# Gamma on GpSimd and VectorE ahead of the root, and three stores instead of four, in the last row block of a matmul with RMS norm

## The chip, the cores and the metric

One core of one Trainium2 chip. The profile is one execution of the program. Its engines are TensorE (PE), VectorE (DVE), ScalarE (ACT), GpSimd (POOL) and SyncE (SP, which here issues stores). In the text, **R** is the start of the last reciprocal in the trace, the moment from which everything still to do is scaling and storing. "R+4.95" is 4.95 us after it. A packet is one piece that a DMA engine moves; a store has landed when its completion has reached its semaphore, the counter that SP waits on. "The root" is the square root of the mean square of a row, and r its reciprocal.

## The reference

```python
m, k, n = 2048, 2048, 2048
x = np.matmul(a, b)
rms = np.sqrt(np.mean(x ** 2, axis=-1, keepdims=True) + eps)
return (gamma * x / rms).astype(np.float32)
```

## The kernel before

The kernel forms the product in groups of two row blocks of 128 rows, with seven block products for each half of the columns in place of eight (a Strassen scheme). A row block can leave only when its whole row of 2048 columns is known, because the root needs the sum of all its squares. For the last block, `rb`, that is after the last matmul, so everything from there to the last byte in the output is exposed. The columns are named by chunks of 512: chunks 0 and 1 are the halves of the tile `xb`, chunk 2 is `p4[1]` (in PSUM, the memory that the matmuls write), chunk 3 is `x22[1]`; `x22[0]` is chunk 1.

```python
        product(g, 0, 6, p6)
        add(x22[0], p6, t[0])                # chunk 1 of the last block
        square(rb, x22[0])
        # ... (first row block is stored here; chunk 2 becomes complete in p4[1])
        for h, col in enumerate(halves):     # chunk 3, in two halves, after the last matmuls
            add(x22[1][:, col], p6[h], t[1][:, col])
            # ... ACT squares this half and sums it into half_sq[:, h]
        part = stat_pool.tile([P, 1], FP32, name="part")
        nc.vector.tensor_scalar(out=part, in0=half_sq[:, 0:1], scalar1=pre_b,
                                scalar2=msq[rb][:, 2:3], op0=ALU.add, op1=ALU.add)
        add(x22[0], x22[0], gam[1], ALU.mult)          # chunk 1 times gamma
        r_b = inverse_rms(half_sq[:, 1:2], part)       # ACT root, VectorE reciprocal
        x = xb[:, 0:CH]
        nc.vector.tensor_scalar_mul(out=x, in0=x, scalar1=r_b)
        nc.sync.dma_start(out=rows(rb, 0, CH), in_=x)
        x = xb[:, CH:]
        by_r(x, r_b)                                   # ACT scales chunk 1
        nc.scalar.dma_start(out=rows(rb, CH, HALF), in_=x)
        for c, x, src in ((3, x22[1], x22[1]), (2, x21[1], p4[1])):
            scaled_gamma(x, src, r_b, gam[c])          # times r and gamma, one operation
            nc.sync.dma_start(out=rows(rb, c * CH, (c + 1) * CH), in_=x)
```

So four stores of 256 KB leave, in rows of 2 KB per partition.

Of the kernel before, what the change touches and what calls it, by code (L numbers as in the profile page):

```python
# [8 lines left out]
FP32 = mybir.dt.float32  # L9
# [4 lines left out]
ALU = mybir.AluOpType  # L14
# [3 lines left out]
def kernel(  # L18
# [13 lines left out]
    nc = tc.nc  # L32
    P = 128
    M, K = a.shape
    _, N = b.shape
# [4 lines left out]
    CH = 512  # L40
    NCH = N // CH
    HALF = N // 2
# [6 lines left out]
    a_pool = ctx.enter_context(tc.tile_pool(name="a_pool", bufs=2))  # L49
# [60 lines left out]
    a32 = {}  # L110
# [156 lines left out]
    def b_quarter(j, kp, r, c):  # L267
        return raw[j][kp][:, r, c * CH:(c + 1) * CH]
# [24 lines left out]
    def product(g, j, m, bank, start=True, within={}):  # L293
        for kp in range(KP):
            for work in within.get(kp, ()):
                work()
            product_matmul(g, j, m, bank, kp, start)
# [5 lines left out]
    def square(mb, src):  # L303
        c = n_sq[mb]
        n_sq[mb] += 1
        sq = sq_pool.tile([P, 2 * CH], BF16, name="sq")
        nc.scalar.activation(out=sq[:, 0:CH], in_=src, func=ACTF.Square,  # L307
                             scale=inv_sqrt_n, accum_out=msq[mb][:, c:c + 1])
# [8 lines left out]
    def x_tile(mb, h):  # L317


        if (mb, h) not in x_half:  # L320
            n = n_x[0]
            n_x[0] += 1
            if n < 8:
                slot = n
            else:
                g = n // 4
                slot = ((0, 4, 1, 5), (0, 1, 4, 5))[g // 2 % 2 == 0][n % 4] + 2 * (g % 2)
            x_half[mb, h] = x_slot[slot]
        return x_half[mb, h]

    def x_chunk(mb, c):
        return x_tile(mb, c // 2)[:, (c % 2) * CH:(c % 2 + 1) * CH]
# [15 lines left out]
    def inverse_rms(last, partial):  # L348

        rms = stat_pool.tile([P, 1], FP32, name="rms")  # L350
        nc.scalar.activation(out=rms, in_=last, func=ACTF.Sqrt, bias=partial, scale=1.0)  # L351
        return inverse(rms)

    def rows(mb, lo, hi):
        return out[mb * P:(mb + 1) * P, lo:hi]
# [18 lines left out]
    def finish(mb, order=(0, 1)):  # L374
        for h in order:
            scale(mb, (h,))
            store(mb, (h,))
# [9 lines left out]
    def new_bank():  # L387
        return ps_a.tile([P, CH], FP32, name="acc")
# [121 lines left out]
    x11, x12, x21, x22 = (x_chunk(r, c) for r in (r2, r3) for c in (2, 3))  # L510
# [47 lines left out]
    def last_squares():  # L558

        while late:  # L560
            square(*late.pop(0))
# [121 lines left out]
    def last_group():  # L683


        g = NG - 1
        ra, rb = 2 * g, 2 * g + 1
        x11, x12, x21, x22 = ([x_chunk(mb, 2 * j + c) for j in range(2)]
                              for mb in (ra, rb) for c in range(2))
        xa, xb = x_tile(ra, 0), x_tile(rb, 0)  # L690
        gam = [gamma_sb[:, c * CH:(c + 1) * CH] for c in range(NCH)]
        gam_left = gamma_sb[:, 0:HALF]
        t = x22

        def partial(mb):

            m = msq[mb]
            part = stat_pool.tile([P, 1], FP32, name="part")
            nc.vector.tensor_scalar(out=part, in0=m[:, 0:1], scalar1=m[:, 1:2],
                                    scalar2=m[:, NCH:], op0=ALU.add, op1=ALU.add)  # L700
            return part

        def plus(part, mb, c):
            both = stat_pool.tile([P, 1], FP32, name="both")
            nc.vector.tensor_tensor(out=both, in0=part, in1=msq[mb][:, c:c + 1], op=ALU.add)
            return both

        def add(out, in0, in1, op=ALU.add):
            nc.vector.tensor_tensor(out=out, in0=in0, in1=in1, op=op)  # L709

        def scaled_gamma(x, src, r, gamma_of_x):
            nc.vector.scalar_tensor_tensor(out=x, in0=src, scalar=r, in1=gamma_of_x,  # L712
                                           op0=ALU.mult, op1=ALU.mult)

        def by_r(x, r):
            nc.scalar.activation(out=x, in_=x, func=ACTF.Copy, scale=r)

        p4 = []
        for j in range(2):
            p5, p1 = new_bank(), new_bank()  # L720
            p4.append(new_bank())
            product(g, j, 5, p5)
            nc.scalar.copy(out=t[j], in_=p5)
            last_squares()
            product(g, j, 1, p1)
            add(t[j], p1, t[j], ALU.subtract)
            if j == 0:
                finish(2 * g - 2)
            product(g, j, 4, p4[j])
            nc.scalar.copy(out=x21[j], in_=p4[j])  # L730
            add(x11[j], t[j], x21[j])
            if j == 0:
                finish(2 * g - 1)
            product(g, j, 3, p5, start=False)
            nc.scalar.copy(out=x12[j], in_=p5)
            square(ra, x12[j])
            add(t[j], x11[j], x12[j])
            p7 = new_bank()
            product(g, j, 7, p7)
            add(x11[j], p7, x11[j])  # L740
            square(ra, x11[j])
            if j == 0:
                product(g, j, 2, p4[j], start=False)
                nc.scalar.copy(out=x21[j], in_=p4[j])
                square(rb, x21[j])
                add(t[j], t[j], x21[j], ALU.subtract)
                pre_a = partial(ra)
                add(xa, xa, gam_left, ALU.mult)
                add(x21[j], x21[j], gam[0], ALU.mult)
        r_a = inverse_rms(msq[ra][:, NCH - 1:NCH], plus(pre_a, ra, 2))  # L750
        by_r(xa, r_a)
        nc.sync.dma_start(out=rows(ra, 0, HALF), in_=xa)
        p6 = new_bank()
        product(g, 0, 6, p6)
        add(x22[0], p6, t[0])
        square(rb, x22[0])
        scaled_gamma(x_tile(ra, 1), x_tile(ra, 1), r_a, gamma_sb[:, HALF:])
        nc.sync.dma_start(out=rows(ra, HALF, N), in_=x_tile(ra, 1))
        product(g, 1, 2, p4[1], start=False)
        add(t[1], t[1], p4[1], ALU.subtract)  # L760
        square(rb, p4[1])
        pre_b = partial(rb)

        half_sq = stat_pool.tile([P, 2], FP32, name="n2")
        halves = [slice(0, CH // 2), slice(CH // 2, CH)]
        p6 = [new_bank()[:, 0:CH // 2] for _ in halves]
        for bank, col in zip(p6, halves):
            for kp in range(KP):
                nc.tensor.matmul(bank, s_sum[6][:, kp, :], b_quarter(1, kp, 0, 1)[:, col],
                                 start=(kp == 0), stop=(kp == KP - 1))  # L770
        for h, col in enumerate(halves):
            add(x22[1][:, col], p6[h], t[1][:, col])
            sq = sq_pool.tile([P, 2 * CH], BF16, name="sq")
            nc.scalar.activation(out=sq[:, 0:CH // 2], in_=x22[1][:, col], func=ACTF.Square,  # L774
                                 scale=inv_sqrt_n, accum_out=half_sq[:, h:h + 1])
        part = stat_pool.tile([P, 1], FP32, name="part")
        nc.vector.tensor_scalar(out=part, in0=half_sq[:, 0:1], scalar1=pre_b,
                                scalar2=msq[rb][:, 2:3], op0=ALU.add, op1=ALU.add)
        add(x22[0], x22[0], gam[1], ALU.mult)
        r_b = inverse_rms(half_sq[:, 1:2], part)  # L780
        x = xb[:, 0:CH]
        nc.vector.tensor_scalar_mul(out=x, in0=x, scalar1=r_b)  # L782
        nc.sync.dma_start(out=rows(rb, 0, CH), in_=x)
        x = xb[:, CH:]
        by_r(x, r_b)
        nc.scalar.dma_start(out=rows(rb, CH, HALF), in_=x)
        for c, x, src in ((3, x22[1], x22[1]), (2, x21[1], p4[1])):
            scaled_gamma(x, src, r_b, gam[c])
            nc.sync.dma_start(out=rows(rb, c * CH, (c + 1) * CH), in_=x)

    for g in range(G0, NG - 1):
        for j in range(2):
            group_half(g, j, hooks_of(g, j))
    last_group()

# [33 lines left out]
```

## Time and profile before

| | before |
|---|---|
| time, median of the first 3 runs | 223.0 us |
| span of the profiled execution, granted TensorE clock | 221.1 us, 0.993 |
| R | 214.59 us |
| last store issued | R+2.03 |
| last data packet ends | R+4.95 |
| last store landed | R+5.53 |
| span end | R+6.51 |

The page's busy times (first line) and the engines of the chain that ended last (second line):

```profile
PE 210.4 (95%) x1035; PEld 97.7 (44%) x1035; DVE 167.9 (76%) x330; ACT 128.0 (58%) x263; POOL 26.7 (12%) x56
...
PE 69%; DMA 23%; DVE 2%; POOL 2%; issue 1%; ACT 1%; DVEq 0%; ACTq 0%; POOLq 0%
```
The kernel is bound by TensorE: 95% busy. The change does not touch that part. What it touches is the last 8 us, seen in the timeline of the kernel before (columns: start, duration, engine, line of the kernel, operation, output<-input, shapes):

```profile
213.16 0.42 DVE L709 TENSOR_TENSOR x<-acc,x 128x256 f32<-128x256 f32 x1 [0.27 <-PE acc L769]
...
213.72 0.27 DVE L777 TENSOR_SCALAR part<-n,part,msq 128x1 f32<-128x1 f32 x1
213.91 0.68 DVE L709 TENSOR_TENSOR x<-x,gamma_sb 128x512 f32<-128x512 f32 x1
...
214.26 0.29 ACT L351 ACTIVATE rms<-n,part 128x1 f32<-128x1 f32 x1
214.59 0.16 DVE L345 RECIPROCAL r<-rms 128x1 f32<-128x1 f32 x1
214.79 0.72 ACT L716 ACTIVATE x<-x,r 128x512 f32<-128x512 f32 x1 [0.23 <-DVE r L345]
214.79 0.48 DVE L782 TENSOR_SCALAR x<-x,r 128x512 f32<-128x512 f32 x1
215.19 0.74 DVE L712 SCALAR_TENSOR_TENSOR x<-x,r,gamma_sb 128x512 f32<-128x512 f32 x1
215.30 0.33 SPq L783 DMA_DIRECT2D out_dram<-x  x1
215.54 0.35 ACTq L786 DMA_DIRECT2D out_dram<-x  x1
215.85 0.74 DVE L712 SCALAR_TENSOR_TENSOR x<-acc,r,gamma_sb 128x512 f32<-128x512 f32 x1
215.96 1.05 SPq L789 DMA_DIRECT2D out_dram<-x  x2
```
The second half of chunk 3 comes out of PSUM at 213.16. ACT squares it, and takes the root at 214.26; VectorE forms the partial sum (L777) and multiplies chunk 1 by gamma (L709, 0.68 us) meanwhile. At 214.59 comes the reciprocal (R). Then VectorE scales chunk 0 in 0.48 us, and chunks 3 and 2 with r and gamma together in 0.74 us each. The stores are issued as these end; the last line merges two, at 215.96 and 216.62.

What the DMA engines do after that, in 40 slices of 0.1 us from R+1.41 (busy share in tenths, then GB/s):

```profile
DMA  0689999999989999999699999999795643100000
GB/s 0 205 328 410 451 369 389 348 349 430 410 184 266 307 410 369 369 307 266 164 266 348 348 389 389 389 287 348 246 328 184 266 184 143 41 0 0 0 0 0
```
None of these stores' packets moves before R+1.54, 0.83 us after the first issue. Then the engines are busy for some 3 us, but the rate dips, to 184, 164 and 246 GB/s between stretches of 350 to 410, and it tails off.

The time from issue to landing in the same stretch (columns: tensors, issuing queue, operation, count, size, median us to landing):

```profile
out_dram<-x SPq DMA_DIRECT2D x3, 256.0 KB, 3.5
out_dram<-x ACTq DMA_DIRECT2D x1, 256.0 KB, 3.1
```

### The profile page before, as it was taken

The numbers are of one execution on the slowest core, as the hardware profiler recorded it, in microseconds if no ns is written. First come the engines' busy times: TensorE is split into PE (matmuls) and PEld (weight loads), VectorE is DVE, ScalarE is ACT, GpSimd is POOL, SyncE is SP. The second block draws the span as 40 slices with busy tenths as digits, with TensorE's granted clock in tenths as the row PEclk, the third lists the DMA queues.
The fourth block names the chain that finished last, engine by engine and source line by source line (L and its number), as shares of the span: only waits on it lengthen the run. The fifth ranks groups of instructions, "written<-read, shape, count | busy, mean of one in ns | idle before, by whom it ended". The sixth has DMA issues, their size and how long they took to land.

```text
span 221.1 us, 3017 instructions
## 1 busy us (share of the span) xinstructions
PE 210.4 (95%) x1035; PEld 97.7 (44%) x1035; DVE 167.9 (76%) x330; ACT 128.0 (58%) x263; POOL 26.7 (12%) x56
## 2 busy tenths in 40 slices
PE   7999999999999999999999999999999999999950
PEld 2445445444455444444444444444444444444430
DVE  2428789999978898969696649855794759797691
ACT  3110002920698898578846997299738995334580
POOL 7534232220000002200100002000200000000000
PEclk9999999999999999999999999999999999999997
DMA  6999999999938595946799149945798349044045
GB/s 184 226 203 210 202 208 211 212 211 240 424 113 354 195 294 107 361 189 175 213 320 409 45 88 269 373 205 95 195 312 348 75 89 386 21 190 193 1 191 190
DMA packets 36464, 47.13 MB, mean 213 GB/s; under 512 B 21984, under 2 KB 26080, under 8 KB 35040
## 3 DMA queue, kind: packets, MB, share of 16 engines
q0 software_dynamic: 9936, 23.33, 41.2%
q1 hardware_dynamic: 26080, 22.29, 33.6%
q10 hardware_dynamic: 432, 1.31, 2.1%
q8 instruction: 8, 0.13, 0.2%
q14 instruction: 8, 0.07, 0.1%
HBM read 34.60 MB, written 16.78 MB: 232 GB/s over the span
## 4 chain that ended last, share of the span: by engine, by line
PE 69%; DMA 23%; DVE 2%; POOL 2%; issue 1%; ACT 1%; DVEq 0%; ACTq 0%; POOLq 0%
PE acc L289 67%; DMA b<-in_b_dram 23%; DVE x L709 1%; POOL early L105 1%; DVE x L712 1%; PE acc L384 1%; POOL b L99 1%; ACT sq L307 0%; PE tbank L189 0%; PE acc L189 0%; DVEq L824 0%; ACT sq L774 0%; DVE x L782 0%; DVE r L345 0%; ACT rms L351 0%
## 5 line engine op out<-in xcount | busy, mean ns | idle before, releaser
L289 PE MATMUL acc<-b,s 128*128 128x512 bf16 x408 | 92.1, 379 | 0.2 <-DMA b<-in_b_dram 0.2
L289 PEld LDWEIGHTS <-s 128*128 128x128 f16 (+1 forms) x512 | 49.9, 98 | 60.3 <-issue 0.5
L384 PE MATMUL acc<-b,head_at 128*128 128x512 bf16 x176 | 41.8, 379 | 0.6 <-DMA b<-in_b_dram 0.5
L307 ACT ACTIVATE sq<-x 128x512 bf16<-128x512 f32 x54 | 34.0, 630 | 6.9 <-DVE x L709 3.0
L366 DVE SCALAR_TENSOR_TENSOR x<-x,r,gamma_sb 128x1024 f32<-128x1024 f32 x28 | 34.8, 1281 | 0.7
L223 ACT ACTIVATE sq<-a 128x1024 bf16<-128x1024 f32 x24 | 25.3, 1054 | 2.5 <-DMA a<-in_a_dram 2.0
L384 PEld LDWEIGHTS <-head_at 128*128 128x128 bf16 x176 | 16.8, 98 | 20.1 <-issue 1.2
L246 ACT ACTIVATE head_at<-a,s 128x2048 f16<-128x2048 f32 x10 | 20.0, 1998 | 3.7 <-DVE s L233 3.7
L426 ACT COPY x<-acc 128x512 f32<-128x512 f32 x6 | 3.4, 588 | 25.2 <-PE acc L384 25.2
L289 PEld LDWEIGHTS <-head_at 128*128 128x128 f16 (+1 forms) x112 | 10.9, 98 | 13.2
L289 PE MATMUL acc<-early,head_at 128*128 128x512 bf16 x64 | 14.5, 379 | 0.0
L289 PEld LDWEIGHTS <-at_even 128*128 128x128 f16 x96 | 9.4, 98 | 11.3
L289 PE MATMUL acc<-early,s 128*128 128x512 bf16 x56 | 14.4, 379 | 0.0
L264 DVE TENSOR_TENSOR s<-head_at 128x1024 f16<-128x1024 f16 (+5 forms) x22 | 13.4, 635 | 0.1
L596 DVE TENSOR_TENSOR x<-x,x 128x512 f32<-128x512 f32 x9 | 6.2, 692 | 8.8 <-ACT x L594 8.3
L99 POOL DMA_DIRECT2D b<-in_b_dram x15 | 10.6, 705 | 15.5 <-DMA b<-in_b_dram 13.0
L578 ACT COPY x<-acc 128x512 f32<-128x512 f32 x9 | 5.2, 573 | 11.5 <-PE acc L289 11.5
L289 PE MATMUL acc<-t_left,s 128*128 128x512 bf16 x48 | 11.3, 379 | 0.0
L280 DVE TENSOR_TENSOR b<-b 128x1024 bf16<-128x1024 bf16 x16 | 10.8, 686 | 0.2
L289 PE MATMUL acc<-t_left,at_even 128*128 128x512 bf16 x48 | 10.8, 379 | 0.0
L289 PE MATMUL acc<-early,at_even 128*128 128x512 bf16 x48 | 10.8, 379 | 0.0
L289 PE MATMUL acc<-t_left,head_at 128*128 128x512 bf16 x48 | 10.8, 379 | 0.0
(106 smaller groups left out, 215.0 us busy)
## 6 DMA issues: line engine op xcount, KB each, us to landing
out_dram<-x SPq DMA_DIRECT2D x30, 512.0 KB, 3.9
a<-in_a_dram POOLq DMA_DIRECT2D x10, 1024.0 KB, 8.6
b<-in_b_dram POOLq DMA_DIRECT2D x15, 512.0 KB, 17.0
a<-in_a_dram POOLq DMA_DIRECT2D x4, 512.0 KB, 17.2
early<-in_a_dram POOLq DMA_DIRECT2D x7, 256.0 KB, 14.6
early<-in_b_dram ACTq DMA_DIRECT2D x2, 512.0 KB, 5.9
gamma_sb<-in_gamma_dram POOLq DMA_DIRECT2D x1, 1024.0 KB, 15.3
out_dram<-x SPq DMA_DIRECT2D x3, 256.0 KB, 3.5
```

Of the source, the lines that this page charges most:

```text
L99: nc.gpsimd.dma_start(out=raw[j][kp], in_=b[kp * W2:(kp + 1) * W2, j * HALF:(j + 1) * HALF].rearrange("(t p) n -> p t n", p=P))
L223: nc.scalar.activation(out=junk, in_=a32[mb][:, h * HALF:(h + 1) * HALF], func=ACTF.Square, scale=2.0 ** -8, accum_out=n2[:, h:h + 1])
L246: nc.scalar.activation(out=a16[mb], in_=a32.pop(mb), func=ACTF.Copy, scale=factor.pop(mb))
L264: nc.vector.tensor_tensor(out=sum_of(g, s)[:, lo:hi, :], in0=x[:, lo:hi, :], in1=y[:, lo:hi, :], op=op)
L280: nc.vector.tensor_tensor(out=flat[:, 1:3, :], in0=flat[:, 1:3, :], in1=flat[:, 0::3, :], op=ALU.add)
L289: nc.tensor.matmul(bank, lhsT[:, kp, :], rhs, start=(start and kp == 0), stop=(kp == KP - 1), skip_group_check=not start)
L307: nc.scalar.activation(out=sq[:, 0:CH], in_=src, func=ACTF.Square, scale=inv_sqrt_n, accum_out=msq[mb][:, c:c + 1])
L366: nc.vector.scalar_tensor_tensor(out=x, in0=x, scalar=inverse_of[mb], in1=gamma_sb[:, h * HALF:(h + 1) * HALF], op0=ALU.mult, op1=ALU.mult)
L384: nc.tensor.matmul(bank, head_at[:, kt, r, :], head_rhs(c, kt), start=(kt == 0), stop=(kt == KT - 1))
L426: copy(out=x_chunk(*g), in_=banks[g])
L578: nc.scalar.copy(out=c, in_=one[1])
L596: nc.vector.tensor_tensor(out=t, in0=t, in1=x12, op=ALU.add)
```

## The change

The intent: have every chunk multiplied by gamma before r is known, so that VectorE has three cheap scalings after the root instead of one cheap and two dear ones; let the idle GpSimd do the multiplications for which VectorE has no time; and let chunks 2 and 3 leave in one store of 512 KB, so that there are three stores, two on SP and the last on ACT.

```diff
         square(rb, x22[0])
+        nc.gpsimd.tensor_tensor(out=x22[0], in0=x22[0], in1=gam[1], op=ALU.mult)
 ...
+        right = a_pool.tile([P, K], FP32, name="a32")[:, 0:HALF]
 ...
             add(x22[1][:, col], p6[h], t[1][:, col])
+            nc.gpsimd.tensor_tensor(out=right[:, CH:][:, col], in0=x22[1][:, col],
+                                    in1=gam[3][:, col], op=ALU.mult)
 ...
-        add(x22[0], x22[0], gam[1], ALU.mult)
+        add(right[:, 0:CH], p4[1], gam[2], ALU.mult)
         r_b = inverse_rms(half_sq[:, 1:2], part)
-        x = xb[:, 0:CH]
-        nc.vector.tensor_scalar_mul(out=x, in0=x, scalar1=r_b)
-        nc.sync.dma_start(out=rows(rb, 0, CH), in_=x)
-        x = xb[:, CH:]
-        by_r(x, r_b)
-        nc.scalar.dma_start(out=rows(rb, CH, HALF), in_=x)
-        for c, x, src in ((3, x22[1], x22[1]), (2, x21[1], p4[1])):
-            scaled_gamma(x, src, r_b, gam[c])
-            nc.sync.dma_start(out=rows(rb, c * CH, (c + 1) * CH), in_=x)
+        by_r(right[:, 0:CH], r_b)
+        nc.vector.tensor_scalar_mul(out=xb[:, 0:CH], in0=xb[:, 0:CH], scalar1=r_b)
+        nc.sync.dma_start(out=rows(rb, 0, CH), in_=xb[:, 0:CH])
+        nc.vector.tensor_scalar_mul(out=right[:, CH:], in0=right[:, CH:], scalar1=r_b)
+        nc.sync.dma_start(out=rows(rb, HALF, N), in_=right)
+        nc.vector.tensor_scalar_mul(out=xb[:, CH:], in0=xb[:, CH:], scalar1=r_b)
+        nc.scalar.dma_start(out=rows(rb, CH, HALF), in_=xb[:, CH:])
```

## The prediction

> **What bounds it now.** Span 221.1 us, median 223.0. The page shows TensorE busy 95% at a granted clock of 0.99; the chain that ended last is 69% TensorE and 23% input DMA. The last matmul ends near 213.1 (timeline), so the change touches only the last 8 us. The chain of waits there: half sums from PSUM (end 213.58), square, partial sum, root (214.26), reciprocal (to 214.75), first VectorE scaling (214.79), then the stores, issued at 215.30 (SP), 215.54 (ACT), 215.96 and 216.62 (SP), as VectorE frees them; its last operation ends at 216.59. In 0.2 us windows the DMA engines move nothing before 216.0, are at a share of about 1.0 from 216.2 to 219.0 and stop by 219.5: 1.05 MB in 3.2 us, 330 GB/s. The last store lands near 220.1; end synchronisation closes the span. So the tail is 0.75 us of store start, then DMA throughput, not compute alone. The 512 KB stores of 211.2 and 212.0 ran at 410 GB/s (4 KB per partition row against 2 KB): smaller pieces cost DMA time.
>
> **What the change does.**
> 1. Before the root VectorE did x22[0]*gamma (0.68 us, 213.91); now p4[1]*gamma from PSUM, the same size: 0.68 us, hidden under the root's chain either way. Neutral.
> 2. GpSimd gets x22[0]*gamma, 512 columns, and two multiplications of 256. The trace has none to measure. From the Trainium skill, "GPSIMD Engine Reference", section 3.1 (4497 ns for a two-input fp32 operation of 2048 elements, about 2.6 cycles an element), I estimate 1.27 and 0.71 us; no run here shows it yet. The first waits for ACT's square of x22[0] (ends 211.8): 211.85 to 213.1; the halves 213.15 to 214.6, about 0.2 us before r.
> 3. After r: VectorE does three scalings of 0.48 us (measured, L782; 0.40 apart) where it did one of 0.48 and two of 0.74 with gamma. It ends at about 216.1 instead of 216.59. ACT keeps one scaling of 0.72 us, of another chunk.
> 4. Stores: 256 KB at 215.3 (unchanged, SP), 512 KB at 215.7 (SP), 256 KB at 216.1 (ACT). The last issue comes 0.5 us earlier, and half the bytes have 4 KB rows.
>
> **Worth.** DMA starts at the same 216.05. Estimate: 524 KB at 410 plus 524 KB at 330 GB/s is 2.9 us against 3.2, so the last landing is near 219.7 instead of 220.1. Gain 0.3 to 0.5 us, all on the critical path, but 0.2% of it. Prediction 222.6 us, 222.1 to 223.2; faster by over 2% 0.01, within 2% 0.97, slower by over 2% 0.02.
>
> **What would show it.** Root and reciprocal at the same times (within 0.1 us); GpSimd multiplications about 1.3 and 0.7 us, done before 214.8; VectorE end near 216.1; stores at 215.3, 215.7, 216.1; 350 GB/s or more from 216.2 to 219; the last landing 0.3 to 0.5 us earlier.
>
> **What would make it wrong.** (a) GpSimd slower than estimated, or its first operation paying a start-up cost: the second scaling waits for it, and stores slip. (b) The port shared with VectorE ("SBUF — State Buffer", "Who interferes with whom": an exclusive lock): the 0.48 us scalings run faster per element than the 0.68 us ones, so are probably two-port operations, blocked by GpSimd's last half if they meet; if the PSUM multiplication or the partial sum is blocked too, the root slips by up to 0.7 us and the gain is gone. (c) If 512 KB beside 256 KB on another queue shares the engines badly, only the earlier issue remains; if the tail is completion latency, the gain is nearer 0.5 us.

## More of the kernel before

Times are device microseconds (us) of one execution.

```profile
SPq L824 <- DMA out_dram<-x: 2.6, 4, 0.7
```

SP waits for the four stores at the end (total us, number, longest). So the end of the kernel is: the stores start, the bytes move, the last one is confirmed, and about 1 us of closing synchronisation follows (R+5.53 to R+6.51).

## The result

The changed kernel took 222.80 us (median of 6, 222.38 to 222.97), the kernel before 222.99 (6 runs of the same rounds, 222.22 to 223.01). The ratio is 0.9995, 95% interval 0.9979 to 1.0011: no difference that these runs can show.

The single runs of each kernel spread over 0.6 and 0.8 us here, more than what is looked for. The traces tell where that comes from: in the fourteen traces R lies between 214.20 and 215.26 us, without order by kernel, whereas the time from the end of the last matmul to R is 1.46 to 1.47 us in every one. The variation lies in the 213 us before, which the change does not touch. Its source was not pursued. Counting from R takes it away; the tail of a kernel then repeats within 0.01 to 0.02 us, as two repeats below show.

The timeline after:

```profile
212.14 1.27 POOL L757 TENSOR_TENSOR x<-x,gamma_sb 128x512 f32<-128x512 f32 x1 [52.55 <-ACT sq L307]
...
213.38 1.41 POOL L775 TENSOR_TENSOR a<-x,gamma_sb 128x256 f32<-128x256 f32 x2
213.38 0.42 DVE L709 TENSOR_TENSOR x<-acc,x 128x256 f32<-128x256 f32 x1 [0.26 <-PE acc L771]
...
213.95 0.27 DVE L781 TENSOR_SCALAR part<-n,part,msq 128x1 f32<-128x1 f32 x1
214.14 0.68 DVE L709 TENSOR_TENSOR a<-acc,gamma_sb 128x512 f32<-128x512 f32 x1
...
214.49 0.29 ACT L351 ACTIVATE rms<-n,part 128x1 f32<-128x1 f32 x1
214.81 0.16 DVE L345 RECIPROCAL r<-rms 128x1 f32<-128x1 f32 x1
215.01 0.72 ACT L716 ACTIVATE a<-a,r 128x512 f32<-128x512 f32 x1 [0.23 <-DVE r L345]
215.01 0.49 DVE L786 TENSOR_SCALAR x<-x,r 128x512 f32<-128x512 f32 x1
215.41 0.48 DVE L788 TENSOR_SCALAR a<-a,r 128x512 f32<-128x512 f32 x1
215.53 0.33 SPq L787 DMA_DIRECT2D out_dram<-x  x1
215.81 0.48 DVE L790 TENSOR_SCALAR x<-x,r 128x512 f32<-128x512 f32 x1
215.97 0.37 SPq L789 DMA_DIRECT2D out_dram<-a  x1
216.32 0.35 ACTq L791 DMA_DIRECT2D out_dram<-x  x1
```
Read it against the one before. GpSimd (POOL) multiplies in 1.27 us, and the two halves in 1.41 us together, and is done at 214.79, as the reciprocal starts (214.81); the product is in place 0.22 us before the first scaling. VectorE's multiplication from PSUM (214.14) takes 0.68 us beside it, as the other one did. After R, VectorE does three operations of 0.48 us, 0.40 apart, and ends at R+1.48 instead of R+2.0. The last store is issued at R+1.51 instead of R+2.03. All of this is as predicted.

The same 4 us of DMA, from R+1.39 (busy share in tenths, then GB/s):

```profile
DMA  0389999999995979999999899999630000000000
GB/s 0 143 328 410 369 430 389 369 492 348 492 328 205 410 287 451 410 410 492 369 410 369 328 369 389 471 348 348 226 103 0 0 0 0 0 0 0 0 0 0
```
The dips are fewer, and the last packet ends at R+4.48 instead of R+4.95. The time to landing, and SP's waits for stores:

```profile
out_dram<-a SPq DMA_DIRECT2D x1, 512.0 KB, 3.1
out_dram<-x SPq DMA_DIRECT2D x1, 256.0 KB, 2.5
out_dram<-x ACTq DMA_DIRECT2D x1, 256.0 KB, 3.8
```
```profile
SPq L826 <- DMA out_dram<-x: 3.4, 2, 2.0
```
The store that comes last, ACT's, needs 3.8 us from issue to landing where the last one of the kernel before needed 3.5. So the gain shrinks on the way to the end. Worked out of the packets, semaphores and waits of the traces:

| in us from R | before | after | gain |
|---|---|---|---|
| last store issued | 2.03 | 1.51 | 0.52 |
| last data packet ends | 4.95 | 4.48 | 0.47 |
| last store landed | 5.53 | 5.28 | 0.25 |
| span end | 6.51 | 6.37 | 0.14 |

0.22 us are lost between the last packet and its landing (0.58 us before, 0.80 after), and 0.11 us between the landing and the end. The second loss is visible in SP's sequence at the end, from the two traces, which SP works off in a fixed order of semaphores:

```
time from R at which SP's wait was over
before: store 1 3.30, store 2 4.10, store 3 4.88, store 4 (last to land) 5.54, one more wait 5.60, drain 5.67
after:  store 1 3.23, store 3 (last to land) 5.29, store 2 5.35, two more waits 5.41 and 5.47, drain 5.54
```

Each wait costs some 0.06 us even where its event is long past. In the kernel before one such wait stood behind the last landing; after the change it is three. One of the two more is the 512 KB store's, since the ACT store's semaphore is checked ahead of it; the other comes of having one store fewer, since the semaphore that the fourth store used is still checked, now behind the stores.

### The profile page after: what moved, and what is told of

It is laid out like the page before. It is cut to its first block, busy times and chain, and to the rows that moved or that the text cites. A ratio compares the mean times of both kernels' runs of the same rounds, so it can differ in the third digit from the quotient of the medians.

```text
span 221.2 us, 3022 instructions
## 1 busy us (share of the span) xinstructions
PE 210.0 (95%) x1035; PEld 97.7 (44%) x1035; DVE 167.4 (76%) x330; ACT 128.1 (58%) x263; POOL 29.4 (13%) x59
## 4 chain that ended last, share of the span: by engine, by line
PE 83%; DMA 8%; POOL 3%; DVE 2%; issue 1%; ACT 1%; DVEq 0%; ACTq 0%; POOLq 0%
PE acc L289 69%; PE acc L384 12%; DMA b<-in_b_dram 8%; POOL early L105 1%; POOL b L99 1%; DVE x L709 1%; PE tbank L415 1%; PE tbank L172 1%; DVE x L712 1%; ACT sq L307 0%; PE tbank L189 0%; PE acc L189 0%; DVE a L709 0%; ACT sq L778 0%; DVE x L786 0%
```

## The experiments

All twelve gave the reference's result. Times are from R; the runs with several rounds also have a ratio to the kernel before.

**How steady is the tail: both kernels again.** The same two kernels, unedited.

> The changed kernel once more, to see how steady its tail is. Times in R are counted from the start of the last reciprocal. First profile: span end at R+6.37 (kernel before: R+6.51), last data packet ends R+4.48 (before R+4.95), last landing R+5.28 (before R+5.53). If the tail is steady, these repeat within 0.05 us, whatever the total does (six runs lay between 222.4 and 223.0). If the small difference of the tails is itself noise, they move by 0.2 us or more.

> The kernel before once more, one look at the steadiness of its tail. Times in R are counted from the start of the last reciprocal. First profile: last packet ends R+4.95, last landing R+5.53, span end R+6.51. Expected within 0.05 us if the tail is steady; by 0.2 us or more apart if the packets that took 116 to 214 ns instead of 86 in it are chance.

Measured: the changed kernel's packets end at R+4.50 (4.48 the first time), last landing R+5.29 (5.28), span end R+6.38 (6.37). The kernel before: R+4.94 (4.95), R+5.53 (5.53), R+6.51 (6.51). So the tails are steady, the gain of 0.14 us repeats (two profiles of each kernel), and even the mean packet time repeats (99 ns before, 86 ns for packets of 2 KB after). The total did not show it: 222.68 us (222.34 to 223.41, 6 runs) against 222.54 (11 runs), ratio 1.0006, interval 0.9990 to 1.0021.

**The queue of the last store.**

```diff
-        nc.scalar.dma_start(out=rows(rb, CH, HALF), in_=xb[:, CH:])
+        nc.sync.dma_start(out=rows(rb, CH, HALF), in_=xb[:, CH:])
```

> Only the queue of the last store changes, from ACT to SP. Theory A (the second queue costs completion time: in both profiles the ACT store landed 0.79 to 0.80 us after its last packet, the SP stores 0.5 to 0.6 after theirs; and SP checks the completions in a fixed order, two more of 0.065 us each after this one): data still end near R+4.5, landing near R+5.0, span end near R+6.1, so 0.25 us less. Theory B (what is left is the time to move the last bytes, whatever the queue): no change, R+6.37 within 0.05.

Measured: packets end R+4.49, last landing R+5.28, span end R+6.33; 222.60 us, ratio 1.0003 (0.9989 to 1.0017). The landing did not move. Theory A is refuted in its main part: the 0.8 us between the last packet and the landing do not come from ACT's queue. Its small part holds: the semaphore of the last store is now checked one place later, one wait fewer stands behind it, and the end comes 0.04 us sooner.

**The merged store alone.** The kernel before, with nothing on GpSimd, and one store for chunks 2 and 3.

```diff
-        for c, x, src in ((3, x22[1], x22[1]), (2, x21[1], p4[1])):
-            scaled_gamma(x, src, r_b, gam[c])
-            nc.sync.dma_start(out=rows(rb, c * CH, (c + 1) * CH), in_=x)
+        scaled_gamma(x22[1], x22[1], r_b, gam[3])
+        scaled_gamma(x21[1], p4[1], r_b, gam[2])
+        nc.sync.dma_start(out=rows(rb, HALF, N), in_=x_tile(rb, 1))
```

> The kernel before with one change: chunks 2 and 3 leave in one 512 KB store after both are scaled; gamma stays after the root on VectorE, nothing on GpSimd. VectorE ends at R+2.0 as before, and the last store is issued there, 0.5 us after the last of the changed kernel. Theory A (the number of stores sets how fast the data go; earlier issue is worth little because the queue is full): data end near R+4.3, landing near R+4.9, span end R+5.9, better than the changed kernel. Theory B (the earlier issue of the last store is what the change gained): data end 0.3 to 0.5 us after the changed kernel's R+4.48, span end at R+6.5 or later.

Measured: last issue R+2.03, packets end R+4.73, last landing R+5.21, span end R+6.24; 222.51 us, ratio 1.0004 (0.9986 to 1.0021). Neither theory had the numbers: the packets end 0.25 us after the changed kernel's, a little less than B had said, but the end comes 0.13 us before it, as A had the sign. The merge alone, without gamma moved at all, is worth 0.27 us of the tail of the kernel before. The last issue at R+2.03 costs less than it seems, and "the last packet" is not the quantity to predict: this store lands 0.48 us after its last packet, the changed kernel's 0.80.

**The merged store cut again.** The changed kernel, with its large store in two.

```diff
-        nc.sync.dma_start(out=rows(rb, HALF, N), in_=right)
+        nc.sync.dma_start(out=rows(rb, HALF, HALF + CH), in_=right[:, 0:CH])
+        nc.sync.dma_start(out=rows(rb, HALF + CH, N), in_=right[:, CH:])
```

> The changed kernel with the 512 KB store cut in two of 256 KB on the same queue, issued one behind the other; four stores as in the kernel before, all rows of 2 KB. If the number of stores costs (packets at the start of a store are slower): data end near R+4.8 instead of R+4.48, packets of 2 KB at a mean near 99 ns as in the kernel before. If only the order and time of issue count: R+4.5, mean 86 ns.

Measured (one look, 222.84 us): packets end R+4.83, packets of 2 KB 96 ns in the mean, last landing R+5.33, span end R+6.33. The first theory holds for the packets: of the 0.47 us by which the change brought their end forward, 0.35 (4.83 less 4.48) come from merging two stores into one, and 0.12 (4.95 less 4.83) from the rest of the change, the earlier issues among it. But the landing comes only 0.05 us later than with three stores, and the span end is the same or slightly earlier, because only one wait follows the last landing. Merging these two stores, in this place, gained almost nothing at the end.

**Small rows without more stores.** The changed kernel with chunks 2 and 3 in places that do not touch, so that its 512 KB store moves pieces of 2 KB. In the output the two pieces of a row still touch.

```diff
-        right = a_pool.tile([P, K], FP32, name="a32")[:, 0:HALF]
+        full = a_pool.tile([P, K], FP32, name="a32")
+        c2, c3 = full[:, 0:CH], full[:, HALF:HALF + CH]     # in place of right[:, 0:CH], right[:, CH:]
 ...
-        nc.sync.dma_start(out=rows(rb, HALF, N), in_=right)
+        nc.sync.dma_start(
+            out=rows(rb, HALF, N).rearrange("p (c n) -> p c n", c=2),
+            in_=full.rearrange("p (c n) -> p c n", c=4)[:, 0::2, :])
```

> The changed kernel, with chunks 2 and 3 kept apart in on-chip memory, so that the one store of 512 KB moves pieces of 2 KB instead of 4 KB. Prediction's theory (small rows go at 330 GB/s instead of 410): data end near R+4.8. Rival (a packet costs the same per byte, 86 ns for 2 KB and 172 for 4 KB in the changed kernel's trace; the count of stores matters, not the rows): no change, R+4.5.

Measured (one look, 223.11 us, with R late at 214.88): all 512 packets of 2 KB, packets end R+4.46, last landing R+5.31, span end R+6.43. The prediction's reason for the faster stream, 4 KB rows, is refuted: with 2 KB pieces the stream ends just as soon. The changed kernel's packets say the same: 173 ns for 4 KB in the mean, 86 ns for 2 KB.

**GpSimd in the way.** The changed kernel with one more GpSimd operation whose result nobody reads.

```diff
+        nc.gpsimd.tensor_tensor(out=full[:, HALF:HALF + CH], in0=x22[1], in1=gam[3], op=ALU.mult)
         part = stat_pool.tile([P, 1], FP32, name="part")     # right is now full[:, 0:HALF]
```

> The changed kernel with one multiplication of 512 columns more on GpSimd, into memory that nobody reads, queued behind the two halves: it should run from R-0.02 to R+1.25, across all three scalings of VectorE. Nothing waits for it. If the port shared by GpSimd and VectorE is held for the whole instruction and the scalings need it: the first scaling ends near R+1.7 instead of R+0.68, its store slips by 1 us, span end near R+7.3. If they do not collide: everything stays within 0.05 us.

Measured (one look, 223.50 us). The timeline of this run, where R is 214.53:

```profile
214.47 1.27 POOL L781 TENSOR_TENSOR a<-x,gamma_sb 128x512 f32<-128x512 f32 x1
...
214.72 1.29 DVE L789 TENSOR_SCALAR x<-x,r 128x512 f32<-128x512 f32 x1
215.93 0.47 DVE L791 TENSOR_SCALAR a<-a,r 128x512 f32<-128x512 f32 x1
216.04 0.33 SPq L790 DMA_DIRECT2D out_dram<-x  x1
```
GpSimd's extra operation runs from 214.47 to 215.74. VectorE's first scaling, which depends on nothing of it, starts at 214.72 and takes 1.29 us instead of 0.49: it ends 0.27 us after GpSimd does. The next one, not disturbed, takes 0.47. The first store slips by 0.8 us and the span end comes at R+7.20, 0.83 us late. This one meeting fits what the Trainium skill, "SBUF — State Buffer", section "Who interferes with whom", says: the pair of ports that the two engines share is locked for a whole instruction, and the other engine waits. It also says that a VectorE instruction with at most one input in SBUF, outside the two-port modes, does not collide; the multiplication from PSUM, with gamma as its one input in SBUF, kept its 0.68 us beside GpSimd, in this run and in the changed kernel, which agrees. In the change as made, GpSimd is clear of the first scaling by 0.22 us.

**Two large stores.** The changed kernel's multiplications; ACT scales chunk 1, VectorE chunks 0, 2 and 3, and the row leaves in two halves on SP.

```diff
-        by_r(right[:, 0:CH], r_b)
+        by_r(xb[:, CH:], r_b)
         nc.vector.tensor_scalar_mul(out=xb[:, 0:CH], in0=xb[:, 0:CH], scalar1=r_b)
-        nc.sync.dma_start(out=rows(rb, 0, CH), in_=xb[:, 0:CH])
+        nc.sync.dma_start(out=rows(rb, 0, HALF), in_=xb)
+        nc.vector.tensor_scalar_mul(out=right[:, 0:CH], in0=right[:, 0:CH], scalar1=r_b)
         nc.vector.tensor_scalar_mul(out=right[:, CH:], in0=right[:, CH:], scalar1=r_b)
         nc.sync.dma_start(out=rows(rb, HALF, N), in_=right)
-        nc.vector.tensor_scalar_mul(out=xb[:, CH:], in0=xb[:, CH:], scalar1=r_b)
-        nc.scalar.dma_start(out=rows(rb, CH, HALF), in_=xb[:, CH:])
```

> The changed kernel's multiplications, with chunk 1 scaled on ACT, chunks 0, 2 and 3 on VectorE, and two stores of 512 KB on SP instead of three on two queues. First issue near R+0.95 instead of R+0.72, second near R+1.5. If two large stores on one queue are served best: data from R+1.7 to R+4.4, landing near R+4.9, span end near R+5.95, 0.4 us under the changed kernel. If the later first issue decides: data end 0.2 us after the changed kernel's, R+4.7, span end R+6.3 or later.

Measured: the first issue comes at R+1.01, the first packet at R+1.83 (changed kernel R+1.54), packets end R+4.59, last landing R+4.94, span end R+6.05; 222.11 us (222.03 to 222.18, 5 runs), ratio 0.9977 (0.9965 to 0.9989). It starts 0.29 us later and lands 0.34 us earlier. No packet in it took over 178 ns for 4 KB, where the changed kernel had some of 312.

**Two large stores without GpSimd.** The kernel before, with only the stores changed.

```diff
-        x = xb[:, 0:CH]
-        nc.vector.tensor_scalar_mul(out=x, in0=x, scalar1=r_b)
-        nc.sync.dma_start(out=rows(rb, 0, CH), in_=x)
-        x = xb[:, CH:]
-        by_r(x, r_b)
-        nc.scalar.dma_start(out=rows(rb, CH, HALF), in_=x)
-        for c, x, src in ((3, x22[1], x22[1]), (2, x21[1], p4[1])):
-            scaled_gamma(x, src, r_b, gam[c])
-            nc.sync.dma_start(out=rows(rb, c * CH, (c + 1) * CH), in_=x)
+        by_r(xb[:, CH:], r_b)
+        nc.vector.tensor_scalar_mul(out=xb[:, 0:CH], in0=xb[:, 0:CH], scalar1=r_b)
+        nc.sync.dma_start(out=rows(rb, 0, HALF), in_=xb)
+        scaled_gamma(x22[1], x22[1], r_b, gam[3])
+        scaled_gamma(x21[1], p4[1], r_b, gam[2])
+        nc.sync.dma_start(out=rows(rb, HALF, N), in_=x_tile(rb, 1))
```

> The kernel before with nothing on GpSimd and gamma after the root for chunks 2 and 3 (two operations of 0.74 us, VectorE ends at R+2.0), but with the stores of the best run so far: two of 512 KB on SP, the first near R+0.95, the second near R+2.05. Theory A (the shape of the stores is what counts; the queue is still full when the second comes): last landing near R+4.95, span end R+6.05, as with gamma on GpSimd; about 0.4 us under the kernel before. Theory B (the earlier end of VectorE, bought with GpSimd, is part of that run's gain): last landing R+5.3 or later, span end R+6.4.

Measured: packets end R+4.52, last landing R+4.87, span end R+5.97; 221.95 us (221.81 to 222.18, 6 runs) against 222.71 of the kernel before in these rounds (222.48 to 223.44, 11 runs), ratio 0.9957 (0.9943 to 0.9971). Theory A holds. The timeline shows what the argument rests on (R is 214.44):

```profile
214.63 0.49 DVE L782 TENSOR_SCALAR x<-x,r 128x512 f32<-128x512 f32 x1
215.04 0.75 DVE L712 SCALAR_TENSOR_TENSOR x<-x,r,gamma_sb 128x512 f32<-128x512 f32 x1
215.38 0.33 SPq L783 DMA_DIRECT2D out_dram<-x  x1
215.70 0.75 DVE L712 SCALAR_TENSOR_TENSOR x<-acc,r,gamma_sb 128x512 f32<-128x512 f32 x1
216.47 0.33 SPq L786 DMA_DIRECT2D out_dram<-x  x1
```
VectorE works until R+2.0, as in the kernel before, and the second store is issued at R+2.03, later than anything in the changed kernel. The DMA stretch, from R+1.36 (busy share in tenths, then GB/s), shows that this costs nothing:

```profile
DMA  0000999999989989899799798998960000000000
GB/s 0 0 0 0 492 410 369 410 410 410 410 328 451 451 369 410 328 451 492 328 451 451 328 410 369 451 492 328 451 246 0 0 0 0 0 0 0 0 0 0
```
The first store keeps the engines busy until about R+3.1, and the second has its first packets ready by then. The stream has no dip below 328 GB/s until its end. Counted from the first issue (R+0.94 here, R+1.01 in the run with two large stores and gamma ahead of the root), the last landing comes some 3.93 us later in both, although the second store is issued 0.5 us later here. So with two large stores, gamma ahead of the root is worth nothing in this kernel: the time it saves is time in which the engines are moving the first half.

The tail is 0.54 us shorter than the kernel before's (6.51 less 5.97). The interval of the total begins at 0.65 us (0.29% of 222.7); the remainder is not seen in the tail of the one profile, and what it is, is open.

**A balanced first half.** The two large stores with gamma ahead of the root, the left half cut at column 704 for VectorE and 320 for ACT, and the right half scaled in one operation. This edit and the next two are shown against the run with two large stores.

```diff
-        by_r(xb[:, CH:], r_b)
-        nc.vector.tensor_scalar_mul(out=xb[:, 0:CH], in0=xb[:, 0:CH], scalar1=r_b)
+        by_r(xb[:, 704:], r_b)
+        nc.vector.tensor_scalar_mul(out=xb[:, 0:704], in0=xb[:, 0:704], scalar1=r_b)
         nc.sync.dma_start(out=rows(rb, 0, HALF), in_=xb)
-        nc.vector.tensor_scalar_mul(out=right[:, 0:CH], in0=right[:, 0:CH], scalar1=r_b)
-        nc.vector.tensor_scalar_mul(out=right[:, CH:], in0=right[:, CH:], scalar1=r_b)
+        nc.vector.tensor_scalar_mul(out=right, in0=right, scalar1=r_b)
```

> The best run so far (two stores of 512 KB on SP, gamma all ahead of the root), with the left half cut at column 704 instead of 512, so that VectorE and ACT end together near R+0.78, and the right half scaled in one operation. First issue about 0.15 us earlier (R+0.8 instead of R+0.95). If the store stream runs at full rate from its start, everything moves with it: landing R+4.8, span end R+5.9. If something else holds the end: R+6.05.

Measured: first issue R+0.92 instead of the hoped R+0.80 (both scalings started at R+0.25 to R+0.27, not R+0.20, and VectorE's took 0.59 us), first packet R+1.75, last landing R+4.86, span end R+5.95; 221.99 us (221.88 to 222.99, 6 runs), ratio 0.9967 (0.9949 to 0.9985). Everything moved with the first issue, by 0.08 us. The size of the gain was missed, the reason held. It is no better than the version without GpSimd.

**Two large stores on two queues.**

```diff
-        nc.sync.dma_start(out=rows(rb, HALF, N), in_=right)
+        nc.scalar.dma_start(out=rows(rb, HALF, N), in_=right)
```

> The best run so far with its second store on the ACT queue instead of SP. If the queue of a store does not matter (as the last store of the changed kernel said): landing R+4.94, span end R+6.05, within 0.06. If a second queue costs: R+6.3.

Measured (one look, 222.28 us): packets end R+4.59, last landing R+4.95, span end R+6.06. The queue does not matter here. This agrees with the Trainium skill, "DMA: Bandwidth & Descriptors", section "Issuing engines are not separate DMA queues": several issuing engines save issue time only.

**Two large stores of split rows.** Two stores of 512 KB on SP, of chunks 0 and 2, then 1 and 3. The scalings write into one new tile, `full`, and ACT scales chunk 2 (these lines are left out).

```diff
+        full_c = full.rearrange("p (c n) -> p c n", c=NCH)          # chunk c at full[:, c * CH:]
+        rows_c = rows(rb, 0, N).rearrange("p (c n) -> p c n", c=NCH)
 ...
-        nc.sync.dma_start(out=rows(rb, 0, HALF), in_=xb)
+        nc.sync.dma_start(out=rows_c[:, 0::2, :], in_=full_c[:, 0::2, :])
 ...
-        nc.sync.dma_start(out=rows(rb, HALF, N), in_=right)
+        nc.sync.dma_start(out=rows_c[:, 1::2, :], in_=full_c[:, 1::2, :])
```

> The best run so far, two stores of 512 KB on SP at the same times, but of chunks 0 and 2, then 1 and 3: each piece is 2 KB in both memories and its neighbours in the output rows belong to the other store. If what made that run good is few large stores: landing within 0.1 of R+4.94, span end R+6.05. If it is whole pieces of 4 KB in the output rows: landing R+5.3 or later, packets of a mean over 90 ns, span end R+6.4.

Measured (one look, 222.88 us): last landing R+5.50, span end R+6.61, which looks like the second answer. But its packets took 88 ns in the mean, none over 126. The store instruction itself took 0.65 us instead of 0.33, and the first packet came at R+2.24 instead of R+1.83. So 0.41 of the 0.56 us by which it lands later are a later start, and 0.15 are the stream. That much the smaller pieces may cost: 88 ns for 2 KB is 175 for 4 KB, where the packets of 4 KB with two large stores took 164 in the mean. The pair of expectations had left out the cost of the start; the stream answers more clearly than the end:

| run (us from R, the last but one column a difference) | stores, KB in order of issue | last issue | first packet | last packet ends | last landing | first packet to last landing | span end |
|---|---|---|---|---|---|---|---|
| before | 256, 256, 256, 256 | 2.03 | 1.54 | 4.95 | 5.53 | 3.99 | 6.51 |
| large store cut again | 256, 256, 256, 256 | 1.61 | 1.54 | 4.83 | 5.33 | 3.79 | 6.33 |
| after | 256, 512, 256 | 1.51 | 1.54 | 4.48 | 5.28 | 3.74 | 6.37 |
| after, all on SP | 256, 512, 256 | 1.61 | 1.54 | 4.49 | 5.28 | 3.74 | 6.33 |
| small rows | 256, 512, 256 | 1.51 | 1.54 | 4.46 | 5.31 | 3.77 | 6.43 |
| GpSimd in the way | 256, 512, 256 | 2.31 | 2.34 | 5.28 | 6.09 | 3.75 | 7.20 |
| merged store alone | 256, 256, 512 | 2.03 | 1.54 | 4.73 | 5.21 | 3.67 | 6.24 |
| two large | 512, 512 | 1.51 | 1.83 | 4.59 | 4.94 | 3.11 | 6.05 |
| two large, two queues | 512, 512 | 1.51 | 1.83 | 4.59 | 4.95 | 3.12 | 6.06 |
| two large, no GpSimd | 512, 512 | 2.03 | 1.77 | 4.52 | 4.87 | 3.10 | 5.97 |
| two large, balanced | 512, 512 | 1.55 | 1.75 | 4.51 | 4.86 | 3.11 | 5.95 |
| two large, split rows | 512, 512 | 1.70 | 2.24 | 5.15 | 5.50 | 3.26 | 6.61 |

The same 1.05 MB need 3.1 to 3.3 us in two stores of 512 KB and 3.7 to 4.0 us in three or four with pieces of 256 KB, whatever the queue, the rows or the time of the last issue. A later start alone does not shorten the stream: with GpSimd in the way it begins 0.8 us later and takes 3.75 us. Two things in the traces make up the difference: packets that take longer in some stretches (up to 226 ns for 2 KB with four stores, against 126 in two split stores), and the time from a last packet to its landing, which is about 0.35 us with two stores and 0.48 to 0.85 with more. Why smaller stores have both is not settled by these runs; count and size changed together.

## Why the prediction was right, and which step of it was not

The predicted 222.6 us (222.1 to 223.2), within 2%, holds against 222.80 and, in the second set of rounds, 222.68 us. That alone tests little: the kernel before, at 222.99, lies in the same range. The mechanism is tested point by point:

- **R not delayed**: right. End of the last matmul to R took 1.46 us before and 1.47 after. The absolute time of R moved by 0.22 us, which belongs to the part of the program that did not change.
- **GpSimd 1.27 and 0.71 us, done just before r**: right. The trace has 1.27 and 0.72 to 0.73 for the two halves; it finished 0.22 us before the first scaling, as against a predicted 0.2. The estimate came from the Trainium skill, "GPSIMD Engine Reference", section 3.1 (4497 ns at 2048 elements, about 2.6 cycles an element); the trace agrees with it. Scaled by columns alone, 4497 ns would have given an estimate of 1.12 and 0.56 us, some 0.15 too low: twice as many columns took 1.27 us and not twice 0.72.
- **VectorE's end and the issues of the stores**: right. The issues came at R+0.72, R+1.16 and R+1.51, predicted R+0.71, R+1.11 and R+1.51.
- **The last packet near 219.0 (216.05 plus 2.9 us), which is R+4.4**: nearly right, R+4.48, but for a wrong reason, so partly by luck; and 0.47 us earlier than before, where the sum (2.9 against 3.2) had 0.3. The rate of the stream came as forecast: 368 GB/s over the 2.8 us that the prediction named, counted from R, against 338 before. The failed step is "524 KB at 410 plus 524 KB at 330 GB/s" with the reason "half the bytes have 4 KB rows". The run with small rows ended its packets at R+4.46, so the rows do not do it; the run with the large store cut again ended them at R+4.83, so the number of stores does, or their size, which changes with it.
- **"So the last landing is near 219.7 instead of 220.1. Gain 0.3 to 0.5 us, all on the critical path"**: mis-sized. The gain is 0.47 us at the last packet, 0.25 at the last landing, and 0.14 at the span end. Two terms were missing from the sum. The landing was taken to follow the last packet after a fixed time, and it went from 0.58 to 0.80 us. And the closing waits were taken as fixed, and went from 0.98 to 1.09 us, since two more checks stand behind the store that now lands last.
- **Danger (b), the shared port**: a true danger that did not happen. Shown by the run with GpSimd in the way, where a 0.49 us scaling took 1.29 us.
- **Danger (c), the two queues sharing the engines badly**: not so. In the changed kernel's trace the ACT store's packets begin as SP's large store runs out (first at R+3.52, SP's last ends at R+3.80); moving the store to SP changed neither packets nor landing. The same point said "if the tail is completion latency, the gain is nearer 0.5 us"; completion time is part of the tail, but it grew with the change, and the gain shrank.

What matters more is behind all of this. The change was made for the earlier end of VectorE. The prediction put it right (step 3) and named the earlier last issue as part of the gain (step 4), though it sized the gain by the stream alone. The run without GpSimd shows that this earlier end is worth nothing once the stores are two large ones, and the run with the merged store alone, with VectorE as slow as before, ended earlier than the whole change (R+6.24 against R+6.37); these two differ also in the place of the large store, last in the one and second in the other.

## What to carry to other kernels

At the end of a kernel, when the last bytes only have to leave, look first at the stores and then at the arithmetic before them: here two stores of 512 KB beat four of 256 KB by 0.5 us although the first left 0.2 us later, and speeding up the arithmetic behind the first store gained nothing as long as that store kept the DMA engines busy. Predict to the last landing and the closing waits, not to the last packet. Where a gain is smaller than the spread of whole runs, count from an event that every trace shows at the same distance from the work in question, and repeat the unchanged kernels to know how steady that measure is.

## What the Trainium skill lacked or had wrong

- "DMA: Bandwidth & Descriptors" has no figure for several stores in a row. The rule in its section "Measured (HBM→SBUF, 128 partitions, SWDGE, issued from GpSimd)", to batch transfers, is about loads, and points the right way: 1.05 MB of stores took 3.1 us from first packet to last landing as 2 x 512 KB, 3.7 us as 256, 512 and 256 KB, and 3.8 to 4.0 us as 4 x 256 KB, with equal time per byte for the changed kernel's packets of 2 and 4 KB (86 and 173 ns in the mean).
- The same page, in "Anatomy of one DMA — SWDGE (gpsimd) path", gives most of a fixed cost of about 2 us to the receipt of the last write; that is for DMAs from GpSimd, and the page has no such figure for stores from SP and ACT. Its section "Latency and other measured facts" adds that a lighter load on the memory makes the cost smaller. Here the time from last packet to landing was not fixed: about 0.35 us in the kernels with two large stores, 0.48 to 0.85 in the others.
- No page tells that a store of two 2 KB pieces per row, separate on the chip and in the output, takes longer to start: the instruction took 0.65 us instead of 0.33, and the first packet came 1.29 us after the issue instead of 0.83. In the run with small rows, where the pieces touch in the output, the instruction took 0.38 us, and 0.37 in the changed kernel.
- No page tells of the program's own closing waits: SP checks the completions in a fixed order, some 0.06 us each, and the span ended 0.98 to 1.12 us after the last landing, the later the more checks (one to three) stood behind it.
- "GPSIMD Engine Reference" and "SBUF — State Buffer" were right where they were used: 1.27 us for a multiplication of 512 columns, and a VectorE scaling held from 0.49 to 1.29 us by a GpSimd instruction.
